# Split GELU-multiply on one core: larger blocks in three rotating buffers, every transfer on one queue

## The chip, the cores and the metric

The kernel runs on 1 core of one Trainium2 chip. The metric is the device time in microseconds; the time before is the median of three runs. Next to it stands one profiled execution, whose trace all views below are taken from.

## The reference

The input x has the shape (32, 512, 2048) in float32, which is 16384 rows of 2048 numbers. Each row is cut in two halves. The first half goes through GELU and is multiplied, number by number, with the second half; the output has 16384 rows of 1024.

```python
half_dim = x.shape[-1] // 2
x1, x2 = (x[..., :half_dim].copy(), x[..., half_dim:].copy())
gelu_x1 = 0.5 * x1 * (1 + erf(x1 / np.sqrt(2)))
return (gelu_x1 * x2).astype(np.float32)
```

The core reads 134.2 MB and writes 67.1 MB.

## The kernel before

The rows are cut into 16 tiles of 1024 rows. In a tile each of the 128 partitions holds R = 8 adjacent rows, so that a tile is one contiguous 8 MB stretch of the input: 64 KB a partition. The output of a tile is 4 MB, 32 KB a partition. Two input buffers (`x_bufs`, 64 KB a partition each) and two output buffers (`o_bufs`, 32 KB each) are used in turn.

Nothing is scheduled by a tool: the program is written out by hand, with its own semaphores. `load` (line 49) issues a load on SyncE's queue. `store` (line 56) first lets its queue wait until every multiply so far is done (`mul_done`), and then issues the store; stores go to ScalarE's queue, except those of the last two tiles, which go to SyncE's.

Per tile, ScalarE waits until the tile's buffer is `ready`, which counts both the load into the input buffer and the earlier store out of the output buffer. It then computes GELU (line 87) in two steps, of 5 and 3 rows, from the first half of each row into the output buffer. VectorE follows step by step (line 95) and multiplies the output buffer in place by the second half of each row. Then ScalarE issues the store, and SyncE, which has waited for the multiplies of this tile, issues the load of the tile two further on into the buffer just read:

```python
if i + 2 < n_tiles:
    nc.sync.wait_ge(mul_done, n[mul_done.name])
    load(i + 2, slice(0, R), ready[k])
```

The first tile is loaded in two halves, and the first and the last tile are computed in steps of 2, 2 and 4 rows and stored in two halves. Ahead of all this ScalarE issues a 4 KB load (line 63) into a scrap buffer that nothing reads.

Of the kernel before, what the change touches and what calls it, by code (L numbers as in the profile page):

```python
# [1 line left out]

# [4 lines left out]

GELU = mybir.ActivationFunctionType.Gelu


@with_exitstack
def kernel(
    ctx: ExitStack,
    tc: tile.TileContext,
    x: bass.AP,
    out: bass.AP,
):
    nc = tc.nc
    P = nc.NUM_PARTITIONS

    x_flat = x.flatten_outer_dims()
    out_flat = out.flatten_outer_dims()
    n_rows, dim = x_flat.shape
    half = dim // 2

    R = 8
    x_t = x_flat.rearrange("(n p r) d -> n p r d", p=P, r=R)
    o_t = out_flat.rearrange("(n p r) d -> n p r d", p=P, r=R)
    n_tiles = x_t.shape[0]
    x_bufs = [nc.alloc_sbuf_tensor(f"x{k}_tile", [P, R, dim], x.dtype) for k in range(2)]  # L30
    o_bufs = [nc.alloc_sbuf_tensor(f"o{k}_tile", [P, R, half], out.dtype) for k in range(2)]

    first = [nc.alloc_semaphore(f"first{j}") for j in range(2)]
    ready = [nc.alloc_semaphore(f"ready{k}") for k in range(2)]
    gelu_done = nc.alloc_semaphore("gelu_done")
    mul_done = nc.alloc_semaphore("mul_done")
    tail_stored = nc.alloc_semaphore("tail_stored")
    opened = nc.alloc_semaphore("opened")  # L40
    scrap = nc.alloc_sbuf_tensor("scrap_tile", [8, 128], x.dtype)
    n = {sem.name: 0 for sem in [*first, *ready, gelu_done, mul_done, tail_stored, opened]}

    def counted(ins, sem, by):
        ins.then_inc(sem, by)
        n[sem.name] += by

    def load(i, rows, sem):
        ins = nc.sync.dma_start(out=x_bufs[i % 2][:, rows, :], in_=x_t[i][:, rows, :])  # L49
        counted(ins, sem, 16)  # L50
        return ins

    def store(queue, i, rows, sem):
        queue.wait_ge(mul_done, n[mul_done.name])
        counted(
            queue.dma_start(out=o_t[i][:, rows, :], in_=o_bufs[i % 2][:, rows, :]), sem, 16
        )

    opening = nc.scalar.dma_start(out=scrap[:, :], in_=x_t[0][:8, 0, :128])
    counted(opening, opened, 16)
    for ins in (
        opening,
        load(0, slice(0, 4), first[0]),
        load(0, slice(4, 8), first[1]),
        load(1, slice(0, 8), ready[1]),
    ):  # L70
        tc.no_tile_sem_insts.add(ins.ins.name)
    tc.close()
    tc.compile()  # L73

    for i in range(n_tiles):
        k = i % 2
        last = i == n_tiles - 1
        pieces = i == 0 or last
        steps = ((0, 2), (2, 4), (4, 8)) if pieces else ((0, 5), (5, 8))
        for lo, hi in steps:  # L80
            rows = slice(lo, hi)
            if i == 0 and lo % 4 == 0:
                nc.scalar.wait_ge(first[lo // 4], 16)
            elif lo == 0:
                nc.scalar.wait_ge(ready[k], n[ready[k].name])
            counted(
                nc.scalar.activation(  # L87
                    out=o_bufs[k][:, rows, :], in_=x_bufs[k][:, rows, :half], func=GELU
                ),
                gelu_done,  # L90
                1,
            )
            nc.vector.wait_ge(gelu_done, n[gelu_done.name])
            counted(
                nc.vector.tensor_mul(  # L95
                    out=o_bufs[k][:, rows, :],
                    in0=o_bufs[k][:, rows, :],
                    in1=x_bufs[k][:, rows, half:],
                ),
                mul_done,  # L100
                1,
            )
            if pieces and hi % 4 == 0:
                if last:
                    store(nc.sync, i, slice(hi - 4, hi), tail_stored)
                else:
                    store(nc.scalar, i, slice(hi - 4, hi), ready[k])
        if not pieces:
            if i == n_tiles - 2:
                store(nc.sync, i, slice(0, R), tail_stored)  # L110
            else:
                store(nc.scalar, i, slice(0, R), ready[k])
        if i + 2 < n_tiles:
            nc.sync.wait_ge(mul_done, n[mul_done.name])
            load(i + 2, slice(0, R), ready[k])


    nc.scalar.wait_ge(opened, 16)
    nc.scalar.drain()  # L119
    for sem in (*first, *ready, opened):  # L120
        nc.scalar.sem_clear(sem)
    nc.vector.drain()
    nc.vector.sem_clear(gelu_done)
    nc.sync.sem_clear(mul_done)
    nc.sync.wait_ge(tail_stored, n[tail_stored.name]).then_inc(
        tail_stored, -n[tail_stored.name]
    )


# [1 line left out]
_INS = ['x']  # L131
_OUTS = [((32, 512, 1024), 'float32')]


# [23 lines left out]
```

## Time and profile before

| | |
|---|---|
| device time, median of 3 runs | 469.25 us (469.18 to 469.42) |
| the profiled execution, its span (first to last instruction) | 467.8 us |
| the profiled execution, what lies around the span | no time of its own is given; the median is 1.4 us over the span |
| busy: VectorE, ScalarE | 140.5 us, 115.5 us |
| moved by DMA | 201.34 MB in 5057 packets, 430 GB/s over the span |
| load of 8 MB, issue to landing (median) | 44.4 us |
| store of 4 MB on ScalarE's queue, issue to landing (median) | 44.7 us |
| one tile in the steady stretch | 29.0 us (GELU starts at 100.40, 129.40, 158.40 us) |

How to read it: the span is that of the program's instructions on the core. A DMA is issued by the queue of an engine (SP is SyncE, ACT is ScalarE, DVE is VectorE), is cut into packets, and lands when the last of 16 DMA engines has counted its semaphore. The time from issue to landing holds the wait behind transfers that were issued before. The share of a DMA window can pass 1.00 a little, since packets at the edges count whole. q1 is SyncE's queue and q10 ScalarE's.

### The profile page before, as it was taken

The numbers are of one execution on the slowest core, as the hardware profiler recorded it, in microseconds if no ns is written. First come the engines' busy times: TensorE is split into PE (matmuls) and PEld (weight loads), VectorE is DVE, ScalarE is ACT, GpSimd is POOL, SyncE is SP. The second block draws the span as 40 slices with busy tenths as digits, with TensorE's granted clock in tenths as the row PEclk, the third lists the DMA queues.
The fourth block names the chain that finished last, engine by engine and source line by source line (L and its number), as shares of the span: only waits on it lengthen the run. The fifth ranks groups of instructions, "written<-read, shape, count | busy, mean of one in ns | idle before, by whom it ended". The sixth has DMA issues, their size and how long they took to land.

```text
span 467.8 us, 154 instructions
## 1 busy us (share of the span) xinstructions
DVE 140.5 (30%) x34; ACT 115.5 (25%) x35; POOL 0.2 (0%) x4
## 2 busy tenths in 40 slices
DVE  0330515207051060511606115060150702507043
ACT  1320606041060410604105050050501506014060
POOL 0000000000000000000000000000000000000000
DMA  8999999999999999999999999999999999999988
GB/s 359 448 448 448 398 406 496 403 403 448 459 437 403 440 412 493 403 403 448 487 409 403 445 406 493 403 403 448 493 403 403 448 426 471 403 426 426 493 384 379
DMA packets 5057, 201.34 MB, mean 430 GB/s; under 512 B 568, under 2 KB 576, under 8 KB 576
## 3 DMA queue, kind: packets, MB, share of 16 engines
q1 hardware_dynamic: 2880, 142.61, 70.6%
q10 hardware_dynamic: 2176, 58.73, 29.1%
q14 instruction: 1, 0.01, 0.0%
HBM read 134.22 MB, written 67.11 MB: 430 GB/s over the span
## 4 chain that ended last, share of the span: by engine, by line
DMA 76%; DVE 14%; ACT 8%; ACTq 0%; SPq 0%; issue 0%
DMA out_dram<-o_tile 66%; DVE o_tile L95 14%; DMA x_tile<-in_x_dram 10%; ACT o_tile L87 8%; ACTq L119 0%; SPq L49 0%
## 5 line engine op out<-in xcount | busy, mean ns | idle before, releaser
L95 DVE TENSOR_TENSOR o_tile<-o_tile,x_tile 128x5120 f32<-128x5120 f32 (+3 forms) x34 | 140.5, 4171 | 319.7 <-ACT o_tile L87 319.7
L87 ACT ACTIVATE o_tile<-x_tile 128x5120 f32<-128x5120 f32 (+3 forms) x34 | 114.3, 3407 | 337.3 <-DMA out_dram<-o_tile 301.8
L87 ACT ACT_TABLE_LOAD x1 | 1.3, 1283 | 2.9 <-PEq L73 2.9
L142 POOL MEMSET const-bfloat16-1.0<- 128x1 bf16 x1 | 0.1, 102 | 0.0
L142 POOL MEMSET const-uint8-127<- 128x1 uint8 x1 | 0.1, 101 | 0.0
L142 POOL MEMSET const-float32-0.0<- 128x1 f32 x1 | 0.1, 99 | 0.2 <-issue 0.2
L142 POOL MEMSET const-float32-1.0<- 128x1 f32 x1 | 0.1, 98 | 0.0
## 6 DMA issues: line engine op xcount, KB each, us to landing
out_dram<-o_tile ACTq DMA_DIRECT2D x13, 4096.0 KB, 44.7
x_tile<-in_x_dram SPq DMA_DIRECT2D x2, 4096.0 KB, 16.7
out_dram<-o_tile ACTq DMA_DIRECT2D x2, 2048.0 KB, 34.4
out_dram<-o_tile SPq DMA_DIRECT2D x1, 4096.0 KB, 25.2
out_dram<-o_tile SPq DMA_DIRECT2D x2, 2048.0 KB, 7.8
x_tile<-in_x_dram SPq DMA_DIRECT2D x15, 44.4
scrap_tile<-in_x_dram ACTq DMA_DIRECT2D x1, 4.0 KB
```

Of the source, the lines that this page charges most:

```text
L87: nc.scalar.activation(out=o_bufs[k][:, rows, :], in_=x_bufs[k][:, rows, :half], func=GELU),
L95: nc.vector.tensor_mul(out=o_bufs[k][:, rows, :], in0=o_bufs[k][:, rows, :], in1=x_bufs[k][:, rows, half:],),
L142: nc = _bacc.Bacc("TRN2", target_bir_lowering=False, num_devices=1)
```

## The change

The tiles become 8 blocks of 2048 rows. In a block each partition holds 16 adjacent rows, 128 KB of input. A block is loaded in two parts, the first 8 rows of every partition and then the last 8: 64 KB a partition each, taken out of every 128 KB. There are three buffers of 64 KB a partition. Part 0 of block b goes to buffer 0 or 2, in turn, and part 1 always to buffer 1.

GELU is computed in place, on the first half of each row. The multiply writes its rows packed into the block's buffer 0 or 2: those of part 0 into its first half, over rows that have been read, those of part 1 into its second half. VectorE therefore also waits for its own previous multiply. Part 0 is computed in steps of 5 and 3 rows, part 1 in steps of 2, 3 and 3. When the block is done, its buffer holds 16 packed rows of 1024, and one store of 64 KB a partition (8 MB in all) writes them out.

All transfers go on SyncE's queue. After the multiplies of block b the queue is given store b, then the load of part 1 of block b + 1; then SyncE waits until store b has landed, since the next load overwrites its buffer, and issues the load of part 0 of block b + 2. For the last two blocks the order is load of part 1 of block 7, store 6, and, after the multiplies of block 7, store 7. The 4 KB scrap load, the half loads and half stores of the first and last tile, and ScalarE's stores are gone.

```diff
     R = 8
-    x_t = x_flat.rearrange("(n p r) d -> n p r d", p=P, r=R)
-    o_t = out_flat.rearrange("(n p r) d -> n p r d", p=P, r=R)
-    x_bufs = [nc.alloc_sbuf_tensor(f"x{k}_tile", [P, R, dim], x.dtype) for k in range(2)]
-    o_bufs = [nc.alloc_sbuf_tensor(f"o{k}_tile", [P, R, half], out.dtype) for k in range(2)]
+    n_blocks = n_rows // (2 * P * R)
+    x_b = x_flat.rearrange("(n p r) d -> n p r d", p=P, r=2 * R)
+    o_b = out_flat.rearrange("(n p r) d -> n p r d", p=P, r=2 * R)
+    bufs = [nc.alloc_sbuf_tensor(f"m{k}_tile", [P, 2 * R, half], x.dtype) for k in range(3)]
 
+    def buf_of(b, part):
+        return 1 if part else 2 * (b % 2)
...
+    def load(b, part):
+        k = buf_of(b, part)
+        rows = bufs[k].rearrange("p (r two) d -> p r (two d)", two=2)
+        ins = nc.sync.dma_start(out=rows, in_=x_b[b][:, part * R : (part + 1) * R, :])
+        counted(ins, ready[k], 16)
         return ins
...
+    def store(b, sem):
+        counted(nc.sync.dma_start(out=o_b[b], in_=bufs[buf_of(b, 0)][:, :, :]), sem, 16)
...
-    opening = nc.scalar.dma_start(out=scrap[:, :], in_=x_t[0][:8, 0, :128])
-    counted(opening, opened, 16)
...
+    for ins in (load(0, 0), load(0, 1), load(1, 0)):
         tc.no_tile_sem_insts.add(ins.ins.name)
...
+    for b in range(n_blocks):
+        for part, steps in ((0, ((0, 5), (5, 8))), (1, ((0, 2), (2, 5), (5, 8)))):
+            k = buf_of(b, part)
+            pairs = bufs[k].rearrange("p (r two) d -> p r two d", two=2)
+            packed = bufs[buf_of(b, 0)][:, part * R : (part + 1) * R, :]
+            nc.scalar.wait_ge(ready[k], n[ready[k].name])
+            for lo, hi in steps:
+                gate = pairs[:, lo:hi, 0, :]
+                counted(nc.scalar.activation(out=gate, in_=gate, func=GELU), gelu_done, 1)
+                if n[mul_done.name]:
+                    nc.vector.wait_ge(mul_done, n[mul_done.name])
+                nc.vector.wait_ge(gelu_done, n[gelu_done.name])
+                counted(
+                    nc.vector.tensor_mul(
+                        out=packed[:, lo:hi, :], in0=gate, in1=pairs[:, lo:hi, 1, :]
+                    ),
+                    mul_done,
+                    1,
+                )
+        nc.sync.wait_ge(mul_done, n[mul_done.name])
+        if b < n_blocks - 2:
+            k = buf_of(b, 0)
+            store(b, ready[k])
+            load(b + 1, 1)
+            nc.sync.wait_ge(ready[k], n[ready[k].name])
+            load(b + 2, 0)
+        else:
+            if b < n_blocks - 1:
+                load(b + 1, 1)
+            store(b, tail_stored)
```

More of the change, by code (lines that the diff above doesn't have):

```diff
@@ L26 @@
     R = 8
-    x_t = x_flat.rearrange("(n p r) d -> n p r d", p=P, r=R)
-    o_t = out_flat.rearrange("(n p r) d -> n p r d", p=P, r=R)
-    n_tiles = x_t.shape[0]
-    x_bufs = [nc.alloc_sbuf_tensor(f"x{k}_tile", [P, R, dim], x.dtype) for k in range(2)]
-    o_bufs = [nc.alloc_sbuf_tensor(f"o{k}_tile", [P, R, half], out.dtype) for k in range(2)]
-    first = [nc.alloc_semaphore(f"first{j}") for j in range(2)]
-    ready = [nc.alloc_semaphore(f"ready{k}") for k in range(2)]
+    n_blocks = n_rows // (2 * P * R)
[4 more added lines that the diff above has]
+        return 1 if part else 2 * (b % 2)
+    ready = [nc.alloc_semaphore(f"ready{k}") for k in range(3)]
     gelu_done = nc.alloc_semaphore("gelu_done")
@@ L39 @@
     tail_stored = nc.alloc_semaphore("tail_stored")
-    opened = nc.alloc_semaphore("opened")
-    scrap = nc.alloc_sbuf_tensor("scrap_tile", [8, 128], x.dtype)
-    n = {sem.name: 0 for sem in [*first, *ready, gelu_done, mul_done, tail_stored, opened]}
+    n = {sem.name: 0 for sem in [*ready, gelu_done, mul_done, tail_stored]}
     def counted(ins, sem, by):
@@ L46, in counted @@
         n[sem.name] += by
-    def load(i, rows, sem):
-        ins = nc.sync.dma_start(out=x_bufs[i % 2][:, rows, :], in_=x_t[i][:, rows, :])
-        counted(ins, sem, 16)
-        return ins
[L53 to L57, printed above, removed]
-    opening = nc.scalar.dma_start(out=scrap[:, :], in_=x_t[0][:8, 0, :128])
-    counted(opening, opened, 16)
[L65 to L70, printed above, removed]
+    def load(b, part):
[3 more added lines that the diff above has]
+        counted(ins, ready[k], 16)
+        return ins
+    def store(b, sem):
+        counted(nc.sync.dma_start(out=o_b[b], in_=bufs[buf_of(b, 0)][:, :, :]), sem, 16)
+    for ins in (load(0, 0), load(0, 1), load(1, 0)):
         tc.no_tile_sem_insts.add(ins.ins.name)
@@ L73 @@
     tc.compile()
[L75 to L115, printed above, removed]
@@ L118 @@
-    nc.scalar.wait_ge(opened, 16)
+    for b in range(n_blocks):
[28 more added lines that the diff above has]
+            store(b, tail_stored)
@@ L119 @@
     nc.scalar.drain()
-    for sem in (*first, *ready, opened):
+    for sem in ready:
         nc.scalar.sem_clear(sem)
```

## The prediction

> **What bounds the kernel now.** I read the page first: the span, the busy shares, and the DMA part.
>
> ```profile
> span 467.8 us, 154 instructions
> ...
> DVE 140.5 (30%) x34; ACT 115.5 (25%) x35; POOL 0.2 (0%) x4
> ...
> DMA packets 5057, 201.34 MB, mean 430 GB/s; under 512 B 568, under 2 KB 576, under 8 KB 576
> ...
> q1 hardware_dynamic: 2880, 142.61, 70.6%
> q10 hardware_dynamic: 2176, 58.73, 29.1%
> ```
>
> No engine is busy for a third of the span, while the two DMA queues together hold 70.6% + 29.1% = 99.7% of what 16 engines can give. The kernel is a stream of bytes. Second, the windows, which ask whether that holds in every phase. Their last two columns are the share of the DMA engines and GB/s.
>
> ```profile
> 3.50:21.50 18.00, 4.49 (x2) 4.35 (x3) 0.00 (x0) 1.00 1.01 435
> ...
> 100.40:419.40 319.00, 96.36 (x22) 78.35 (x22) 0.00 (x0) 1.00 1.00 434
> ...
> 448.80:456.06 7.26, 4.80 (x3) 6.92 (x3) 0.00 (x0) 1.00 1.00 433
> 457.30:464.60 7.30, 2.88 (x1) 0.00 (x0) 0.00 (x0) 1.00 1.00 430
> ```
>
> Loads alone (first row), both kinds mixed (second, eleven tiles of 29.0 us) and stores alone (third and fourth) all run at a share of 1.00 and 430 to 435 GB/s. What differs is packet size: 16 KB packets in the last row, 32 KB in the rows of 433 and 435, 64 KB and 32 KB in turn in the mixed row. Third, the chain that ended last, to see what the share of DVE and ACT in it means:
>
> ```profile
> 113.70 44.67 DMA out_dram<-o_tile
> 158.37 0.02 issue
> 158.40 4.48 ACT o_tile L87
> 162.87 0.02 issue
> 162.90 8.77 DVE o_tile L95 x2
> 171.67 0.02 issue
> 171.69 44.69 DMA out_dram<-o_tile
> ```
>
> The chain passes through 13 us of compute for each 45 us of DMA, but a pair (load and store) is in flight for 44.7 us while one lands every 29.0 us: one pair always stands behind another, so the DMA engines work through that compute. Shortening it gains nothing while the queues hold work.
>
> **The unit of the sum: one packet.** The trace's DMA packet records show one packet for each partition and transfer, 8 on each of 16 engines. On one engine the next packet starts 2.414 us after a 64 KB one, 1.209 us after a 32 KB one (load or store alike), 0.607 us after a 16 KB one. Two halves cost 2.418 us against 2.414 whole: about 4 ns a packet beside its bytes. A completion packet costs some 6 ns (1.215 us from the last 32 KB store packet to the next store's first).
>
> Before, per engine: 15 full loads of 8 packets make 120 x 2.414 = 289.7 us. The two half loads and 14 full stores make 16 + 112 = 128 x 1.209 = 154.8 us. The four half stores make 32 x 0.607 = 19.4 us. 36 completions add 0.2 us. Together 464.1 us. The first load packet starts at 1.74 us and the last packet ends at 467.37 us, 465.6 us apart. The missing 1.5 us are the staggered start and slow first packet of the engines (together 1.0 us for the last engine, whose first packet ends at 3.96) and about 0.45 us of small slips, nearly all before 85 us, where the second queue's first packets come in. From the last packet to the end of the span 0.47 us pass, and the median of 469.25 us lies 1.4 us over the span. I carry both over.
>
> **The change part by part.**
>
> *Packets.* After: 24 transfers of 8 packets of 64 KB: 192 x 2.414 = 463.5 us, plus 24 completions (0.15 us), 463.6 us. Against 464.1 that is **-0.45 us**. The bytes are the same, so this is all that bigger packets can give. The 0.45 us of slips can vanish (one queue, nothing comes in beside it) or recur at the first stores: 0 to -0.45, and I take half, -0.2. Sum: **-0.65 us, 468.6 us**.
>
> *One queue.* For each block SyncE waits for all five multiplies, issues store b and load (b+1, second half), waits for store b to land, then issues load (b+2, first half). Two waits stand in front of the stream, and each is free while the packets already queued outlast it. Their cover is one transfer, 8 x 2.414 = 19.3 us. The groups, kept apart by shape, price the first wait:
>
> ```profile
> L87 ACT ACTIVATE o_tile<-x_tile 128x3072 f32<-128x3072 f32 x14 | 38.5, 2747 | 0.0
> L95 DVE TENSOR_TENSOR o_tile<-o_tile,x_tile 128x2048 f32<-128x2048 f32 x4 | 9.0, 2288 | 32.4 <-ACT o_tile L87 32.4
> ...
> L95 DVE TENSOR_TENSOR o_tile<-o_tile,x_tile 128x3072 f32<-128x3072 f32 x14 | 46.9, 3351 | 0.0
> ...
> L87 ACT ACTIVATE o_tile<-x_tile 128x2048 f32<-128x2048 f32 x4 | 7.4, 1901 | 30.6 <-DMA out_dram<-o_tile 21.9 <-DMA x_tile<-in_x_dram 8.7
> ```
>
> A second half is computed in steps of 2, 3 and 3 rows. ACT ends at 1.90, 4.65 and 7.40 us after landing. The multiplies end at 1.90 + 2.29 = 4.19, then 4.65 + 3.35 = 8.00, then 11.35 us. DVE's new wait for its own previous multiply adds at most the overlap now seen (5.49 + 3.35 - 8.76 = 0.08 us) for each of two, so 11.5 us. Landing trails the last packet by 0.6 us (447.9 to 448.49), and an issue reaches its first packet in 1.0 us (0.73 to 1.74). So the store's first packet is ready 11.5 + 0.6 + 1.0 = 13.1 us after the second half's data, while the load (b+2, first half) behind it fills 19.3 us: **6.2 us to spare**, in every block and, by the same order, at the start and at the end (store 6 covers the computing of block 7). The second wait needs 0.6 + 1.0 = 1.6 us under the 19.3 us of load (b+1, second half). So both waits cost nothing. If the first lost its cover, each us would count for 8 blocks.
>
> *The rest.* GELU in place with rows 2048 apart, and the packed output, leave element counts unchanged: bounded between the same time and 6 us more a half before it shows. No trace row has this access, and the nearest rows (same sizes, contiguous) speak for the same time. First half: 4.47 + 5.49 + 3.35 = 13.3 us, with 38 us until the second half lands. Dropping the 4 KB opening load removes 25 ns packets at 1.69 us, at nothing; were it warming the path, the first load packets could lose a few tenths, and they already take 1.6 to 2.06 us against 1.21. ScalarE's queue loses 15 store issues of 0.36 us, off the path.
>
> *The end.* Now the last multiply ends at 460.2 us and the last packet at 467.4. After, the last store has 8 MB, queued 6 us before store 6 is through: same landing, no gap.
>
> **Rivals.**
>
> *Loads at twice the pitch are slower (chance 0.14, slower).* A load now takes 64 KB out of every 128 KB, where it took a contiguous 8 MB. If addresses so spaced share memory channels, 128 load packets an engine (309 us) stretch. The rows speak against it: packets of 32 KB go at 1.209 us both when they leave every second 32 KB out (the first tile's half loads) and when contiguous (the stores). No row has a 128 KB pitch. It decides from 0.3%: 0.9 us. A stretch of 1% gives +3.1 us, 471.7 us. The Trainium skill, DMA: Bandwidth & Descriptors, section Latency and other measured facts, has a row on pitch that speaks against this change: 207 GB/s a direction at 512 KB against 214 at full, falling further at larger powers of two. By its 3%, an estimate for four times our pitch, loads would take 9 us more. No trace here shows such a loss.
>
> *A load behind a store in one queue waits for the store to finish writing (0.09, slower).* This order is new: in 6 places a load follows a store. At the landing lag of 0.6 us each it costs 3.6 us: 472.2 us. Against it: store behind store in one queue loses 6 ns.
>
> *The first wait loses its cover (0.05, slower).* If the in-place access or the self-wait lengthened the 13.1 us past 19.3, each us beyond counts 8 times: 1 us over gives 476.6 us. It would take compute half again as slow.
>
> *All slips vanish (0.15, faster).* The whole 0.45 us goes, as does the late engine at the end (it ends at 467.37, most by 467.1): -0.45 - 0.45 - 0.1 = -1.0 us, 468.2 us.
>
> *The packets do not grow (0.05, no change).* Were a packed store still cut into 32 KB packets, 64 more packets at 4 ns give back 0.25 us: 469.0 us.
>
> **How the numbers follow.** Forecast, stream stays full, 468.4 to 468.8 us: chance 0.52. A measurement of this kernel tells from no change about 0.2%, 0.94 us, so the forecast is "the same" (-0.14%), as is the fifth rival: 0.57. Faster, under 468.3: 0.15. Slower, over 470.2: 0.14 + 0.09 + 0.05 = 0.28. The range goes from 468.1, a little under the floor, to 471.8, which takes in 1% on the loads and leaves out the larger prices, some 0.15.
>
> **What would show it.** Right: 3072 data packets, a DMA share of 1.00 in every window between 4 and 465 us, a block every 57.9 us (24 x 2.414), and SyncE's stores issued some 6 us before the load in flight is through. Wrong: windows under 430 GB/s that hold only loads (pitch), a dip after each store (second rival), or idle DMA slices just before each store (cover lost).

## The result, and the profile after

The changed kernel takes 472.88 us (median of 6 runs, 471.70 to 472.94) against 469.33 us before (median of 6, one of them at 471.31): a ratio of 1.0064, 95% interval 1.0050 to 1.0079. It is slower by 3.55 us, where 0.65 us less had been forecast. The runs stand at two levels, 471.7 and 472.9; the profiled execution took 472.92 us, with a span of 471.6 us.

First the page of the changed kernel: span, busy engines and DMA.

```profile
span 471.6 us, 191 instructions
...
DVE 142.9 (30%) x40; ACT 116.0 (25%) x41; POOL 0.2 (0%) x4
...
DMA packets 3457, 201.34 MB, mean 427 GB/s; under 512 B 384, under 2 KB 384, under 8 KB 384
...
q1 hardware_dynamic: 3456, 201.33, 99.3%
```

The packets are as forecast: 3072 of 64 KB and 24 x 16 completions, in one queue that is busy for 99.3% of the span. The same bytes nevertheless took longer. Next the windows of the changed kernel, with the DMA share and GB/s in the last two columns.

```profile
100.40:419.40 319.00, 99.80 (x29) 84.98 (x30) 0.00 (x0) 1.00 1.00 432
464.00:466.00 2.00, 0.00 (x0) 0.00 (x0) 0.00 (x0) 1.00 0.76 328
466.00:468.00 2.00, 0.00 (x0) 0.00 (x0) 0.00 (x0) 1.00 1.06 459
468.00:470.00 2.00, 0.00 (x0) 0.00 (x0) 0.00 (x0) 1.00 0.31 131
```

In the long middle the share is 1.00 as before, but at 432 GB/s where it was 434. A packet that is drawn out counts as busy, so the share can't show the loss. At the end (shares are coarse there, since a window counts a packet where it starts) the engines no longer stop together. By the packet records, the last packets of the 16 DMA engines ended between 466.93 and 467.37 us before, and end between 468.47 and 471.22 us now. The chain of the changed kernel gives the time of a block:

```profile
101.30 4.57 ACT m_tile L68 x2
...
112.75 0.34 SPq L53
...
159.66 4.57 ACT m_tile L68 x2
...
218.05 4.57 ACT m_tile L68 x2
...
276.84 4.57 ACT m_tile L68 x2
...
335.17 4.57 ACT m_tile L68 x2
...
393.99 4.57 ACT m_tile L68 x2
```

A block takes 58.3 to 58.8 us instead of the 57.9 of its packets. The start of GELU waits for the last engine's landing, so it follows the slowest engine.

Where the time sits is seen packet by packet. A 64 KB packet takes 2418 ns in the records (the next starts after 2414). Here is the excess over that, summed over the 8 packets of a transfer, as mean over the engines and as the largest, for the loads just before a store in the queue:

| load before | store 0 | 1 | 2 | 3 | 4 | 5 | 6 |
|---|---|---|---|---|---|---|---|
| mean excess, ns | 1201 | 338 | 93 | 511 | 474 | 407 | 130 |
| largest, ns | 1379 | 554 | 330 | 835 | 658 | 904 | 340 |

Nearly all of it lies in the last packet of the load, the one with the store behind it. (The 904 holds 0.6 us in the packet behind a program fetch of 8 KB, which that engine carried at 343.6 us.) Stores themselves stay at 2418 ns, and so do nearly all other loads: their means are 0 to 0.05 us, with up to 0.5 us on a single engine, but for the program's first load, where the first packet of an engine is 0.2 to 0.85 us long. The seven means add up to 3.2 us.

### The profile page after: what moved, and what is told of

It is laid out like the page before. It is cut to its first block, busy times and chain, and to the rows that moved or that the text cites. A ratio compares the mean times of both kernels' runs of the same rounds, so it can differ in the third digit from the quotient of the medians.

```text
span 471.6 us, 191 instructions
## 1 busy us (share of the span) xinstructions
DVE 142.9 (30%) x40; ACT 116.0 (25%) x41; POOL 0.2 (0%) x4
## 3 DMA queue, kind: packets, MB, share of 16 engines
q1 hardware_dynamic: 3456, 201.33, 99.3%
## 4 chain that ended last, share of the span: by engine, by line
DMA 74%; DVE 11%; ACT 7%; ACTq 1%; SPq 1%; issue 0%; DVEq 0%
DMA m_tile<-in_x_dram 74%; DVE m_tile L73 11%; ACT m_tile L68 7%; ACTq L91 1%; SPq L53 0%; SPq L48 0%; DVEq L71 0%
## 5 line engine op out<-in xcount | busy, mean ns | idle before, releaser
L73 DVE TENSOR_TENSOR m_tile<-m_tile 128x3072 f32<-128x3072 f32 (+2 forms) x40 | 142.9, 3572 | 301.5 <-ACT m_tile L68 300.9
L68 ACT ACTIVATE m_tile<-m_tile 128x3072 f32<-128x3072 f32 (+2 forms) x40 | 114.7, 2924 | 321.3 <-DMA m_tile<-in_x_dram 321.3
## 6 DMA issues: line engine op xcount, KB each, us to landing
out_dram<-m_tile SPq DMA_DIRECT2D x8, 27.8
```

What stands on the lines that cost most here:

```text
L68: counted(nc.scalar.activation(out=gate, in_=gate, func=GELU), gelu_done, 1)
L73: nc.vector.tensor_mul(out=packed[:, lo:hi, :], in0=gate, in1=pairs[:, lo:hi, 1, :]),
```

## Experiments

A *step* below is a place in a queue where a store follows a load. "Ends" are the first and the last of the 16 engines' last packets, in the profiled execution. Ratios are to the kernel before, run in the same round.

**Undo one part: stores on ScalarE's queue.** Blocks, buffers and packets stay.

```diff
-        counted(nc.sync.dma_start(out=o_b[b], ...), sem, 16)
+        queue = nc.scalar if b < n_blocks - 2 else nc.sync
+        queue.wait_ge(mul_done, n[mul_done.name])
+        counted(queue.dma_start(out=o_b[b], ...), sem, 16)
```

> The changed kernel with one thing undone: stores 0 to 5 go to ScalarE's queue, stores 6 and 7 stay on SyncE's. Blocks, buffers, 64 KB packets and the 128 KB pitch stay. Theory A (a store that follows a load in a queue that runs alone delays the load's last packet by 0.1 to 1.2 us an engine, and the engines drift apart): the excess at six of the seven places goes, the engines end within about 0.6 us of each other, time 468.3 to 469.3 us. Theory B (the larger blocks, the pitch of 128 KB or the 64 KB stores cost the time): unchanged, 471.7 to 472.9 us. Theory C (what comes late into an almost drained queue is fetched late): the loads' queue is also fed late, about 19 us ahead instead of 6, so it goes as theory A here.

Measured: 475.08 us (472.14 to 477.94), ratio 1.0123 (1.0076 to 1.0169); ends 471.3 to 473.7. My theory failed here. At store 0 the load packet ahead of it was again 0.9 to 1.3 us long on every engine; at stores 1 to 3 next to nothing was lost; then the loads ran late, and at stores 4 and 5 load packets were long once more, by 0.4 to 2.0 and 0.7 to 1.35 us on nearly every engine. Stores on a queue of their own thus don't take the long packets away. SyncE's waits in this run, and in the changed kernel behind it:

```profile
SPq L48 <- DMA out_dram<-m_tile: 257.6, 6, 44.5
SPq L48 <- DVE m_tile L75: 143.5, 7, 50.5
```

```profile
SPq L53 <- DVE m_tile L73: 240.4, 7, 50.6
SPq L48 <- DMA out_dram<-m_tile: 162.8, 6, 28.1
```

A store that takes turns with loads lands later (waits of up to 44.5 us instead of 28.1), and the load of part 0 waits for it. One engine fell 2 to 3 us behind, store 3 landed between 269.5 and 272.9 us, and the next load, issued at 272.89, found the queue of the early engines run dry. So this is no plain test of the queue; the transfers without waits, below, are.

**One part alone: the kernel before with its stores on SyncE's queue.**

```diff
-                    store(nc.scalar, i, slice(hi - 4, hi), ready[k])
+                    store(nc.sync, i, slice(hi - 4, hi), ready[k])
...
-                store(nc.scalar, i, slice(0, R), ready[k])
+                store(nc.sync, i, slice(0, R), ready[k])
```

> The kernel before with one part of the change alone: all its stores go to SyncE's queue, each ahead of the load that waits for the same multiplies. Tiles of 8 rows, 32 KB stores and the two halves stay. Theory A (load then store in one queue): 15 such places instead of 7, at 0.3 to 0.5 us each, and drift: 473 to 478 us. Theory B (blocks, pitch, packets): 469.3 us, as before. Theory C (late feeding): a store here is issued some 14 us ahead of its turn instead of 6, so little or nothing: 469 to 470 us.

Measured: 474.80 us (473.90 to 475.50), ratio 1.0116 (1.0101 to 1.0131). One queue alone makes the old tiles slower than the whole change does. Two things mix: long packets at the steps (1.0 to 1.6 us on every engine at the first, then 0 to 1.1), which draw the engines up to 5 us apart, and, from 458.3 us on, a queue that runs empty for 2.3 to 2.9 us on eleven engines. The second follows from the first: the last load landed at 448.96 us on the first engine and at 453.79 on the last, GELU of the last tile waits for the last (it starts at 453.81), and the early engines were through with the store before by 458.3.

**Less computing, so an earlier store.**

```diff
-        for part, steps in (..., (1, ((0, 2), (2, 5), (5, 8)))):
+        for part, steps in (..., (1, ((0, 2),))):
```

> The changed kernel with less computing: of a second half only the first 2 rows go through GELU and the multiply (the other 6 are left out, so that what is stored there is not the product). The store of a block is issued 7.2 us earlier, some 13 us ahead of its turn instead of 6. Theory A (order of load and store in one queue): the last packet of each load before a store stays long, 471.5 to 473 us. Theory C (late feeding): the excess goes, 468.3 to 469.3 us. Theory B: 471.7 to 472.9 us.

Measured: 471.72 us (470.99 to 472.11), ratio 1.0050 (1.0035 to 1.0065): the 1.1 us at store 0 stay, the later means are 0.02 to 0.19 us. The time lies in the range of theory A, the shorter excess speaks in part for theory C, and the interval overlaps that of the changed kernel.

**The store queued long ahead.** This settles lateness: the second halves are not computed, and the store does not wait for them.

```diff
+        for part, steps in (..., (1, ())):
...
             store(b, ready[k])
+            nc.sync.wait_ge(ready[1], n[ready[1].name])
             load(b + 1, 1)
```

> The changed kernel with the second halves not computed and the store not waiting for them (what is stored of them is not the product): a store is queued as soon as the first half is multiplied, 24 us ahead of its turn at block 0 and over 30 us later, instead of 6. The next second-half load waits for the one before it to land, which is long past. Lateness (theory C, in part borne out by the shorter excess of 13 us ahead): all excess goes, engines end within 0.6 us, 468.3 to 469 us. Theory A alone (order of load and store): 0.1 to 0.2 us at each of the seven places as with 13 us, and 1.1 at the first: 470.5 to 472 us.

Measured: 472.86 us (471.89 to 473.31), ratio 1.0073 (1.0058 to 1.0088), as slow as the changed kernel, with 1.0 us at store 0, means of 0.1 to 0.3 us later and ends of 467.7 to 471.2. The DMA issues of this run show the lead, a store standing queued for most of the 58.0 us it takes to land (27.8 in the changed kernel):

```profile
m_tile<-in_x_dram SPq DMA_DIRECT2D x16, 40.1
out_dram<-m_tile SPq DMA_DIRECT2D x8, 58.0
```

So it is not late feeding.

**A load in the store's place.**

```diff
-            store(b, ready[k])
+            again = bufs[k].rearrange("p (r two) d -> p r (two d)", two=2)
+            counted(nc.sync.dma_start(out=again, in_=x_b[b][:, 0:R, :]), ready[k], 16)
```

> The changed kernel in which stores 0 to 5 are left out and a load of the same size (the block's own first half once more, into the same buffer) stands in the queue in the place of each, issued at the same instant behind the same wait. Stores 6 and 7 stay. Theory A (it is the step from a load to a store): the long last packets go, but for the one before store 6, 467.8 to 469 us. Theory C (late feeding, whatever comes): the excess stays, 471.5 to 473 us. Theory B (pitch): as slow or slower than the changed kernel, 472 to 474 us.

Measured: 469.86 us (469.44 to 470.26), ratio 1.0011 (1.0002 to 1.0021), with all waits, issues, sizes and the pitch as in the changed kernel. No load has a mean excess over 0.07 us except the program's first. That holds for the load before store 6 too, a step that is left in this run and at which the forecast still had a long packet. Fifteen engines end at 466.6 to 466.9, the sixteenth, which carried the program fetch at 341.2 us, at 467.88; in that execution this engine alone accounts for the 0.9 us by which the time lies over the forecast. Windows of this run, against those of the changed kernel above:

```profile
100.40:419.40 319.00, 102.76 (x29) 85.41 (x30) 0.00 (x0) 1.00 1.00 434
464.00:466.00 2.00, 0.00 (x0) 0.00 (x0) 0.00 (x0) 1.00 1.21 524
466.00:468.00 2.00, 0.00 (x0) 0.00 (x0) 0.00 (x0) 1.00 0.00 0
```

434 GB/s are back, and no packet starts after 466 us. So it is not the waits, the issues or the bytes that cost, but the stores that stand between the loads.

**Pitch, addresses, a first store.** Three runs with one edit each:

```diff
+            in_=x_c[2 * b + part]                       # e5: contiguous 8 MB a load
+            out=o_b[b if b >= n_blocks - 2 else 0]      # e6: stores 0 to 5 write one place
+            nc.scalar.dma_start(out=o_b[0][:16, 0, :], in_=bufs[0][:16, 0, :])   # e9
```

> The changed kernel with the pitch undone: each load takes a contiguous stretch of 8 MB, 64 KB a partition, instead of 64 KB out of every 128 KB, so that rows land in other places of the output than they should; the rest is the same. Pitch rival (loads at twice the pitch are slow): 468.3 to 469 us. Theory A (a store queued behind a load): as the changed kernel, 471.5 to 473 us, with the long packets in the same places.

> The changed kernel in which stores 0 to 5 all write the place of block 0, so that blocks 1 to 5 of the output stay unwritten. If a store pays for touching output that was not written yet, the excess before store 0 stays (1.1 us) and that before stores 1 to 5 goes: 469.3 to 470.3 us. If it is the step from load to store, all stay: 471.5 to 473 us.

> The changed kernel with a store of 64 KB (one row of 16 partitions, one packet an engine) on ScalarE's queue at 36 us, ahead of store 0, which writes the same rows again after it has landed. If the 1.1 us before store 0 are the price of the first store of the program, the small store pays them or a part (its packet stands between loads), and the packet before store 0 is long by 0.1 to 0.5 us as at the other places: 471 to 472.5 us, if the small store's price is hidden 0.7 us less. If it is store 0's own price: 1.1 us stay there, 471.7 to 473 us.

Measured: 472.89 (ratio 1.0076, 1.0061 to 1.0091), 472.34 (1.0063, 1.0046 to 1.0080) and 472.65 us (1.0072, 1.0057 to 1.0087). All are as slow as the changed kernel, with the long packets in the same places and 1.0 to 1.2 us at store 0. No cost of the pitch of 128 KB shows, nor of output that was not yet written, and a small store beforehand prepays nothing.

**Transfers alone, and the number of steps.** The kernel's 16 loads and 8 stores without any computing, in one queue; only a load waits, until the load two before it, which goes to the same place, has landed; the first store also waits for its buffer to be zeroed.

```diff
+        for _ in stores:          # m1: eight steps; m4: all loads, then all stores
+            load()
+            load()
+            store()
```

> Transfers alone: the 16 loads and 8 stores of the changed kernel, of 8 MB in 64 KB packets, in the order load, load, store on SyncE's queue. GELU and multiply are left out and the stores write zeros from a buffer of their own, so that nothing waits for computing or for a store. Floor from the packets: 468.3 us. Theory A (each step from a load to a store in one queue costs an engine 0.1 to 0.5 us, 1.1 the first, and the end is set by the slowest engine): 471 to 473 us, as the changed kernel. If the cost came from the waits, the in-place multiply or the packed buffer: 468 to 469 us.

> As the run with eight steps, in the order of all 16 loads and then all 8 stores: one step from load to store. Theory A: the floor and one first step of 1.1 us, 468.5 to 469.8 us, with the engines' ends within 0.7 us. Theory D (long phases): as slow as eight steps or slower, 471 to 474 us.

> As the run with eight steps, but each transfer is cut into four of 2 MB, in the order load, load, store throughout: 32 steps from load to store in one queue instead of 8, in phases a quarter as long. Its packets are 16 KB, so the floor is 3.2 us higher (768 packets of 0.607 us and 96 completions an engine): 471.5 us. Theory A (a price for each step): 32 x 0.3 = 9.6 us over it and drift, 479 to 485 us. Theory D (the price hangs on the length of the phases in which all engines only read or only write): 471.5 to 474 us.

> As the run with 32 steps, with the stores on ScalarE's queue, held back so that they run beside the loads of their turn. If the price of a step is that of one queue: the floor of 16 KB packets, 471.5 us, to 472.5. If stores beside loads cost it in any queue: as the run with 32 steps in one queue.

> Transfers of 8 MB in the order of four loads and two stores: 4 steps, floor 468.3 us. A fixed price: between one step (469.8) and eight (472.7), 470.3 to 471.5 us. A price that grows with the phases: as eight steps or more, 472 to 474 us.

> The same with transfers of 4 MB: 16 steps, packets of 32 KB, floor 469.3 us. A fixed price of 0.3 us a step with 1.1 for the first: 474 to 476.5 us. A price that shrinks with the phases: as eight steps or less, 470.5 to 473 us.

> The 32 steps once more (transfers of 2 MB, load, load, store, one queue, no computing), the store buffer zeroed in four parts so that the first store no longer holds up the queue. Floor of its 16 KB packets 471.5 us. A fixed price of 0.3 us a step: 479 to 484 us. A price that shrinks with the phases: 472.5 to 477 us.

These runs start their first packet at 2.4 us instead of 1.7, so the floors stated ahead of them are 0.7 us low; the run with one step serves as the floor. Smaller packets add 0.9 us (384 x 1.209 and 48 completions an engine against 463.6) and 3.1 us (768 x 0.607 and 96).

| run | time, us | packets | over one step | ends, us |
|---|---|---|---|---|
| one step | 469.79 | 64 KB | 0 | 467.1 to 467.6 |
| 4 steps | 471.68 | 64 KB | 1.9 | 468.0 to 469.3 |
| 8 steps | 472.67 | 64 KB | 2.9 | 468.5 to 471.1 |
| 16 steps | 475.19 | 32 KB, +0.9 | 4.5 | 469.3 to 473.7 |
| 32 steps | 477.33 | 16 KB, +3.1 | 4.4 | 471.5 to 474.7 |
| 32, two queues | 474.81 | 16 KB, +3.1 | 1.9 | 471.3 to 472.1 |

Eight steps and one step, with the same loads and stores, differ by 2.9 us: it is their order that costs. Against the forecasts, eight steps and one step came in as theory A had them (though its 1.1 us for the first step did not come in the run with one), and 16 steps as a fixed price had it; 4 steps, 32 steps repeated, and two queues fell into none of the stated ranges. Eight steps without computing give the time of the changed kernel, so the in-place GELU, the packed multiply and the waits have no share in it. The windows of the run with one step (first fence) and with eight (second) show the ends:

```profile
100.40:419.40 319.00, 0.00 (x0) 0.00 (x0) 1.00 1.00 434
464.00:466.00 2.00, 0.00 (x0) 0.00 (x0) 1.00 1.21 524
466.00:468.00 2.00, 0.00 (x0) 0.00 (x0) 1.00 0.00 0
```

```profile
100.40:419.40 319.00, 0.00 (x0) 0.00 (x0) 1.00 1.00 433
464.00:466.00 2.00, 0.00 (x0) 0.00 (x0) 1.00 0.60 262
466.00:468.00 2.00, 0.00 (x0) 0.00 (x0) 1.00 1.13 492
468.00:470.00 2.00, 0.00 (x0) 0.00 (x0) 1.00 0.23 98
```

Up to 16 steps the price rises with their number, from 16 to 32 it doesn't, and the packet size changes there too. No step has a fixed price: eight times the steps, from 4 to 32, is 2.3 times the price. Of the packets corrected as above, the median engine ends 1.4 to 1.8 us after that of the run with one step, whether there are 4 steps or 32; the last engine 1.7, 3.5, 5.2 and 4.0 us after. So there are two parts: about 1 us on every engine at the first step (0.9 to 1.4 us for the mean engine from 4 steps on), and, from 8 steps on, a few engines that fall behind from step to step and set the end. In two queues that take turns all along, the long packets of the first store remain (some 1.3 us an engine at 20 to 24 us) and the engines stay within 0.8 us. The first run with 32 steps, 484.50 us, had its queue empty for 7 us while the first store waited for the zeroing of its buffer, and tells nothing; the repetition took that out.

**The same 8 MB transfers in two queues.**

```diff
-    TWO = False  # stores on ScalarE's queue
+    TWO = True  # stores on ScalarE's queue
```

> The transfers of the run with eight steps, 8 MB in 64 KB packets, with the stores on ScalarE's queue; a store is held back until the load two before has landed, so its packets go in turn with those of loads, and loads run alone for a third of the time. If only the order within one queue costs: 468.5 to 469.8 us. If a store that comes in beside loads alone costs too (the changed kernel with its stores on ScalarE's queue showed long packets at three of six such places): 470.5 to 473 us.

Measured: 476.64 and 477.69 us in two executions (ratio 1.0170, 1.0150 to 1.0190), 487.39 and 489.68 us in two others. All four are slower than one queue (472.67) and over both forecasts. The trace is that of 487.39, and what follows is shown for it alone. Its windows:

```profile
20.00:340.00 320.00, 0.00 (x0) 0.00 (x0) 1.00 1.00 430
340.00:420.00 80.00, 0.00 (x0) 0.00 (x0) 1.00 1.01 423
420.00:460.00 40.00, 0.00 (x0) 0.00 (x0) 1.00 0.98 388
460.00:486.00 26.00, 0.00 (x0) 0.00 (x0) 1.00 0.61 262
```

Engines came up to 34 us apart in the landing of one load (410.5 to 444.5 us), with long packets in the middle of transfers too. A second queue is therefore no cure by itself. In the kernel before and in the run with 32 steps in two queues, loads and stores are both pending nearly all the time, and their packets alternate; here, and with the changed kernel's stores on ScalarE's queue, loads run alone for a part of each block. That this is the reason was not tested.

**Half of the engines set back.** Eight loads of 64 KB, over 8 partitions each, which half of the engines carry, behind the first load: in the run with eight steps, and in the kernel before.

```diff
+                for j in range(8):
+                    counted(nc.sync.dma_start(out=late[8 * j : 8 * j + 8, :],
+                            in_=x_b[0][8 * j : 8 * j + 8, 0, :]), lagged, 16)
```

> The run with eight steps (load, load, store in one queue, no computing) with 8 small extra loads behind the first load that only half of the engines carry: 8 packets of 8 KB, which set these engines back by 2.5 us. If each engine pays for its own switch, both halves pay alike, and the end moves by the 2.5 us: 474.5 to 476 us, with the late half's and the early half's long packets alike (the first 1.1 to 1.5 us, then 0 to 0.5). If a load packet is slow while other engines store, the late half pays at every step, some tenths to 2 us, and the early half next to nothing, also at the first step; the gap between the halves grows from 2.5 us: 476 to 485 us.

> The kernel before with the same 8 extra loads behind its first half load, so that half of the engines run 2.5 us behind the other half, reading while those write. If reading beside the other engines' writing costs in itself: well over 471.8 us (469.3 + 2.5), 474 us or more, and growing gaps. If it takes one queue's order of load and store: 471.6 to 472.2 us, with the gap of 2.5 us kept to the end.

Measured: 476.13 (475.23 to 476.89) and 474.86 us (473.69 to 475.79). The extra loads came at the pace of their issue and cost every engine more than reckoned: they put one half back by 5 us and the other by 3, so the times can't be set against the forecasts. The traces can. In one queue, in the profiled execution (475.23), no engine lost anything at any of the eight steps, the first included: stores land 57.96 to 58.01 us apart on the first and on the last engine, the packets' own time, and the gap of 2.8 us stays 2.8 from 84 to 473 us. In the kernel before, the gap between the halves (4.2 us) stays the same from 130 to 440 us. In these two traces, reading beside the writing of others thus cost nothing in itself, and being late did not make an engine fall further behind. Both readings that I had offered fail. With the halves apart, the price was gone in that execution; the slower runs may have paid up to 1.7 us of it.

## Why the prediction was wrong

**Packets (-0.45 us).** The count was right, 192 of 64 KB an engine, and so was the gain: with loads in the stores' places fifteen engines end at 466.6 to 466.9, against 466.9 to 467.4 before. The step that failed is that every packet costs 2.414 us *whatever stands next to it*: the order load, store was put at nothing. That row was taken from a kernel whose loads and stores alternate in two queues. In the changed kernel the last load packet before a store took up to 1.3 us more, and the loads ahead of the seven stores 3.2 us in all for the mean engine.

**The sum of one engine.** The second term that was missing is the spread, which the sum carried over from before. It took one engine for all; the end is that of the slowest. The mean of the ends moved from 467.1 to 469.6 (+3.3 us of long packets, less the 0.45 us and some slips), and the slowest was 0.3 us behind the mean before and is 1.6 us behind it now. Together that is 2.5 + 1.4 us, the 3.85 us by which the last packet moved from 467.37 to 471.22 (to rounding).

**The waits.** Right. The first store was issued at 53.42 us and the load ahead of it ended at 61.6, so its first packet, 1.0 us after the issue, had about 7 us to spare against the 6.2 worked out. On the engine that is ahead the spare falls to 4.7 us at store 5 (issued at 346.61, load through at 352.31), since computing starts with the last engine's landing; no engine's queue ran empty. The groups of the changed kernel stand at the durations used, in place and packed:

```profile
L73 DVE TENSOR_TENSOR m_tile<-m_tile 128x3072 f32<-128x3072 f32 x24 | 80.6, 3358 | 3.4 <-ACT m_tile L68 2.9
L68 ACT ACTIVATE m_tile<-m_tile 128x3072 f32<-128x3072 f32 x24 | 65.2, 2747 | 0.0
```

**The rivals.** Pitch: refuted, by the loads' own packets and by the run with contiguous loads. There is thus no loss here from the rule of the Trainium skill, DMA: Bandwidth & Descriptors, section Latency and other measured facts, at 128 KB; its figures begin at 512 KB. A load behind a store: it had the mechanism the wrong way round. A load behind a store loses next to nothing (means of 0 to 0.04 us); it is the load *ahead* of a store that is drawn out. Its price, 3.6 us, is near the measured 3.55 by luck, for the wrong reason, and I gave it 0.09 since store behind store lost 6 ns, a row that shows neither order. Lost cover, vanishing slips, split packets: none came.

**The chances.** 0.28 for slower and a high end of 471.8 us: the time lies 1.1 us over it. The trace of before did hold a hint that I put among the slips: the first 64 KB load packet beside the first store, at 21.7 us, was 0.1 to 0.45 us long on fifteen of the sixteen engines.

**Open.** What happens in a DMA engine, or in memory, when a store comes up behind loads. No change of lead, address, pitch or computing took the long packets away; loads in the stores' places did, and all loads ahead of all stores did nearly. One queue isn't needed for them: with the changed kernel's stores on ScalarE's queue they came at stores 0, 4 and 5, and in the 32 steps in two queues at the first store. Nor is it a fixed price of the order: one step at 310 us cost six engines 0.1 to 0.35 us and the other ten nothing, the step before store 6 in the run with loads in the stores' places cost nothing, and eight steps with the engines in two groups cost nothing. Why a few engines fall behind is open as well. No version that was run beats the kernel before.

## What to carry to other kernels

A DMA share of 1.00 says that the queues hold work, not that the work runs at its rate: compare GB/s, the length of single packets and the spread of the engines' last packets. A packet's cost from one arrangement of loads and stores is not its price in another; here loads and stores alternating packet by packet from two queues lost some 0.25 us, at the first store, and in one queue, a whole load at a time, some 3 us in 470. In a kernel that streams, add a term for the slowest DMA engine: in the changed kernel it ended 1.6 us behind the mean, and nothing brought the engines back into step while the queues held work.

## What the runs showed of the hardware

- A packet has a fixed part of about 4 ns: 0.607, 1.209 and 2.414 us for 16, 32 and 64 KB, loads and stores alike, at 434 GB/s over 16 engines.
- A program fetch of 8 KB falls on a single DMA engine and set it back by about 1 us at 341 us in the run with loads in the stores' places, enough to move the end of the program, and by 0.4 us at 460 us in the kernel before.
- With 8 MB transfers in two queues, loads alone for a part of the time, the engines came 34 us apart in an execution of 487.39 us; two other executions of the same kernel took 476.64 and 477.69 us, and one queue 472.67.
